# Sliding attention: the two key triangles selected by GpSimd from one ScalarE copy

## The chip, the cores and the metric

The kernel runs on one core of a Trainium2 chip. A core has five engines, each with a queue of its own that it works off in order: TensorE (PE in the profile; its weight loads are shown as PEld), VectorE (DVE), ScalarE (ACT), GpSimd (POOL) and SyncE (SP, which here only starts DMAs). They meet through semaphores. SBUF is the working memory of 128 partitions; PSUM is where TensorE writes, and GpSimd does not read it in this kernel. The metric is the device time of one execution in microseconds, as the median of several runs.

## The reference

Two residual layers over 256 tokens of width 1024. Each layer projects the normalised stream with one large matrix and feeds three parallel mixers: a state-space scan, a sliding-window attention and a forgetting attention. Their outputs are gated, projected, merged and added to the stream. The change sits in the sliding-window attention. Its queries come in blocks of 128, and each block sees the block of keys before it and its own:

```python
qi = jnp.arange(blk)[:, None]
sj = jnp.arange(2 * blk)[None, :]
diff = qi + blk - sj
band = (diff >= 0) & (diff < SWA_WINDOW)
key_pos = jnp.arange(nb)[:, None, None] * blk - blk + sj[None]
mask = band[None] & (key_pos >= 0)
scores = jnp.where(mask[None, :, None, None], scores, -jnp.inf)
probs = jax.nn.softmax(jnp.concatenate([scores, sink], axis=-1), axis=-1)[..., :-1]
out = jnp.einsum('bnkgqs,bnskd->bnqkgd', probs.astype(v.dtype), vb)
```

With a window of 128 and blocks of 128, the second query block (b = 1) sees a strict triangle of the first key block and the complementary triangle of the second. Together they are exactly 128 keys a query, so the kernel can hold the probabilities of both triangles in one 128x128 square per head.

## The kernel before, in words

**The dense work.** Everything is float32. A large product is made from three: the operands are split into a high part, rounded by ACT to a format that TensorE takes at a higher rate (`hi`, line 293), and a remainder that DVE computes from it (`lo`, line 294, which reads the raw tile and `hi`, both in SBUF). Weights arrive by SP's DMAs of 512 KB into `raw`, are split, and are then multiplied. Results leave PSUM by ACT copies (lines 489 and 490), whose two halves are added by a DMA that POOL issues (line 491, called from `dma_sum`). On DVE the convolution's taps are line 832, and lines 839 and 940 finish gates; all three read two operands in SBUF. On POOL, line 1071 selects a triangle of the forgetting attention's bias.

**The order.** TensorE's order is written out: the program lists its dense products one after the other, and a small planner (`pump`, with a model clock and the due times in the `D_` constants) enters steps of the attention between them. The order on ACT, DVE and POOL is set by the scheduler that builds the program from the data's dependences.

**The sliding attention.** In each layer four groups of four heads go through `attn_quad` with `window=True`. TensorE makes the scores; DVE and ACT make the softmax, and leave the probabilities in `pps[0]` for the first query block and in `pps[1]` for the second. Then the `if window:` part transposes each block on TensorE (line 113), four heads into one PSUM bank `pt`:

- for b = 0, ACT copies the bank into `first[:, 0, :]` (line 676);
- for b = 1, DVE multiplies the bank by `other`, a strict lower triangle of ones, into `first[:, 1, :]` (line 678), and by `tri`, the upper triangle with the diagonal, into `both` (line 679).

`first` holds both query blocks' weights on the first key block, `both` the second query block's weights on the second key block. `products_with_values` multiplies them with the values: per head one product of 256 columns from `first` and one of 128 from `both`. It is done for two groups at once: `pair` collects them, and `values` runs the first group's products into a bank `mx` and the second group's into a bank `mm`. The values tile stands as `bias` in the profile, since it shares that tile's slots. The selects' or masks' results of the first and third group thus wait for the second and fourth.

The lines of the profile are those of this kernel; behind the change, every line from 209 on stands 3 lower (491 becomes 488, 294 becomes 291).

Of the kernel before, what the change touches and what calls it, by code (L numbers as in the profile page):

```python
# [13 lines left out]
AF = mybir.ActivationFunctionType  # L14
ALU = mybir.AluOpType

P = 128
# [33 lines left out]
def hybrid_trunk(  # L51
# [5 lines left out]
    nc = tc.nc  # L57
# [11 lines left out]
    def T(tag, shape, dtype=F32, bufs=None):  # L69
        count[0] += 1  # L70
        return sb.tile(shape, dtype, tag=tag, name=f"{tag}_{count[0]}",
                       bufs=bufs if bufs is not None else BUFS.get(tag, 1))
# [8 lines left out]
    def pmx():  # L81
        return PS("mx", 5)

    act = nc.scalar.activation
    stt = nc.vector.scalar_tensor_tensor
    tt = nc.vector.tensor_tensor
# [24 lines left out]
    def transpose(o, a, i):  # L111
        clock["t"] += 0.109
        nc.tensor.transpose(o, a, i)  # L113
# [74 lines left out]
    for j in range(2):  # L188
# [3 lines left out]
    tri = T("tri", [P, P])  # L192
    nc.gpsimd.memset(tri, 1.0)
    nc.gpsimd.affine_select(out=tri, in_=tri, compare_op=ALU.is_ge, fill=0.0, base=0,
                            pattern=[[1, P]], channel_multiplier=-1)
# [3 lines left out]
                            pattern=[[1, P]], channel_multiplier=-1)  # L199
# [3 lines left out]
    nc.gpsimd.tensor_copy(onesr, one)  # L203
    ones = onesr.bitcast(F32)

    wmask, other = T("wmask", [P, P]), T("other", [P, P])
    nc.gpsimd.memset(wmask, 0.0)
    nc.gpsimd.affine_select(out=wmask, in_=wmask, compare_op=ALU.is_ge, fill=NEG, base=0,
                            pattern=[[-1, P]], channel_multiplier=1)
    nc.gpsimd.memset(other, 1.0)  # L210
    nc.gpsimd.affine_select(out=other, in_=other, compare_op=ALU.is_ge, fill=0.0, base=-1,
                            pattern=[[-1, P]], channel_multiplier=1)
    mhalf = T("mhalf", [P, 8])
    nc.gpsimd.memset(mhalf, -0.5)
# [5 lines left out]
    def bc(ap, axis, n):  # L220
        s = list(ap.shape)
        s.insert(axis, n)
        return ap.unsqueeze(axis).to_broadcast(s)
# [117 lines left out]
    first, late = [], []  # L341
# [244 lines left out]
    def attn_quad(y, last, products, biases, nsink, v, vcols, sz, gated, scored=lambda: None, window=False):  # L586
# [16 lines left out]
        def score(p, i, b):  # L603
            return scs[2 * p + i][:, b * P:P + 2 * P * b]
# [11 lines left out]
        for h in range(4) if window else ():  # L616
            own = pps[0][:, h // 2, h % 2 * P:h % 2 * P + P]
            nc.vector.tensor_tensor_reduce(  # L618
                out=own, in0=scs[h][:, 0:P], in1=wmask, scale=-0.125, scalar=nsink[:, h:h + 1],
# [23 lines left out]
        for p in () if window else range(2):  # L643
            pp = pps[p]
            ps_ = slice(4 * p, 4 * p + 4)
            for i in range(2):
                for b, sl in blocks:
                    e = 4 * p + 2 * i + b
                    nc.vector.tensor_tensor_reduce(  # L649
                        out=pp[:, i, sl], in0=score(p, i, b), in1=biases(p, i, b), scale=-0.125,  # L650
# [15 lines left out]
        if window:  # L666
            first, both = T("L4", [P, 2, 512]), T("L2", [P, 512])
            for b in range(2):
                if b == 1:
                    yield D_SOFT2  # L670
                pt = pmx()
                for h in range(4):
                    transpose(pt[:, h * P:(h + 1) * P], pps[b][:, h // 2, h % 2 * P:h % 2 * P + P], ident)
                ptv = pt.rearrange("p (h q) -> p h q", h=4)
                if b == 0:
                    act(first[:, 0, :], pt, AF.Copy)
                else:
                    tt(first[:, 1, :].rearrange("p (h q) -> p h q", h=4), ptv, bc(other, 1, 4), op=ALU.mult)
                    tt(both.rearrange("p (h q) -> p h q", h=4), ptv, bc(tri, 1, 4), op=ALU.mult)
        else:  # L680
            order = [(0, 0), (0, 1), (1, 0), (1, 1), (0, 2), (1, 2),
                     (2, 0), (2, 1), (2, 2), (3, 0), (3, 1), (3, 2)]
            at = {hb: (n // 4, n % 4 * P) for n, hb in enumerate(order)}
            pTs = []
            for n, (h, b) in enumerate(order):
                if n == 6:
                    yield D_SOFT2
                if n % 4 == 0:
                    pt = pmx()
                transpose(pt[:, n % 4 * P:(n % 4 + 1) * P], pps[h // 2][:, h % 2, b * P:(b + 1) * P], ident)  # L690
                if n % 4 == 3:
                    if n == 3:
                        two = T("L4", [P, 2, 512])
                    pT = T("L2", [P, 512]) if n == 11 else two[:, n // 4, :]
                    act(pT, pt, AF.Copy)
                    pTs.append(pT)
# [42 lines left out]
    def swa_quad(y, g, q):  # L739
        yield lambda: 1 in y.sz  # L740

        def products(score):
            for b in range(2):
                for c in range(2):
                    for h in range(4):
                        r = slice(32 * h, 32 * h + 32)
                        mm(score(h // 2, h % 2, b), q[r, c, b * P:(b + 1) * P], y.kT[r, (h - g) % 4, c, 0:(b + 1) * P],
                           start=(c == 0), stop=(c == 1))

        yield from attn_quad(  # L750
            y, g == 3, products, None, y.nsink[:, 4 * g:4 * g + 4], y.bv,
            lambda p, i: slice(64 * g, 64 * g + 64),
            lambda: y.sz[1][:, 2 * g:2 * g + 2, :], lambda: (1, 2 * g + 1) in y.zdone, window=True)
# [304 lines left out]
    def fox_quad(y, j):  # L1058
# [26 lines left out]
        def scored():  # L1085
            tokens["bias"] += 1

        yield from attn_quad(y, j == 6, products, lambda p, i, b: bs[p][:, i, P * b:P + 2 * P * b], None, y.cv,
                             lambda p, i: slice(P * (j + p) + 64 * i, P * (j + p) + 64 * i + 64),
                             lambda: y.sz[2][:, j:j + 2, :], lambda: (2, j + 1) in y.zdone, scored)  # L1090
# [168 lines left out]
    def sub(src, n=256):  # L1259
        subs.append((src, n))  # L1260
        return len(subs) - 1
# [5 lines left out]
    for y in layers:  # L1267
# [108 lines left out]
        o = [sub([(0, w_out[l, :, c:c + n])], n) for c, n in ((0, 256), (256, 512), (768, 256))]  # L1376
# [43 lines left out]
    with tc.manual_schedule(engines={ENG.PE, ENG.DVE, ENG.Activation, ENG.Pool}):  # L1420
# [11 lines left out]
        p = pmx()  # L1432
# [93 lines left out]
        for i in range(2):  # L1526
# [6 lines left out]
                                op=ALU.add)  # L1533
# [50 lines left out]
```

## Time and profile before

| what | value |
|---|---|
| median of 3 runs | 808.11 us (807.27 to 808.14) |
| the profiled execution, its own time | 808.24 us |
| its span (first to last instruction) | 806.5 us |
| granted TensorE clock | 0.999 |
| PE busy | 797.2 us (99%) |
| DVE busy | 684.8 us (85%), 1414 instructions |
| ACT busy | 533.7 us (66%), 1144 instructions |
| POOL busy | 170.9 us (21%), 238 instructions |

A row of a timeline has the start and the duration in microseconds, the engine, the line, the operation, output<-inputs, sizes, and the number of instructions merged into it; in brackets stands how long the engine was idle before it and what ended that. A row of a line's own view has shortest, median and longest duration in nanoseconds, and the first and last start. A row of waits has the total, the number of waits and the longest. Matmuls overlap, so their durations are longer than the time from one to the next.

### The profile page before, as it was taken

The page shows a single profiled execution, that of the slowest core. Times are in us where ns is not written, and L with a number is a line of the kernel's source. Part 1 is how long each engine was busy: PE and PEld are TensorE (multiplying, and loading weights), DVE is VectorE, ACT ScalarE, POOL GpSimd, SP SyncE. Part 2 cuts the span into 40 slices and gives each one's busy share as a digit, 9 for nine tenths or more (in the row PEclk, how much of TensorE's full clock was granted, in tenths as well). Part 3 has the DMA queues.
Part 4 walks back from the last instruction along what each step waited for, and adds up shares of the span by engine and source line. Part 5 has one row for each costly group of instructions (what it writes and reads, how often), then busy time and mean ns, then how long its engine had stood idle before and what let it go on. Part 6 is the DMA issues. An engine that isn't in the chain of part 4 may idle for free.

```text
span 806.5 us, 14832 instructions
## 1 busy us (share of the span) xinstructions
PE 797.2 (99%) x5162; PEld 711.2 (88%) x5162; DVE 684.8 (85%) x1414; ACT 533.7 (66%) x1144; POOL 170.9 (21%) x238
## 2 busy tenths in 40 slices
PE   8999999999999999999999999999999999999996
PEld 7998988888888988888998899888889989888896
DVE  6868999998899997795785799999879999969865
ACT  7776768875776785543665678687747768755452
POOL 3156213130320100033001741222212110002000
PEclk9999999999999999999999999999999999999999
DMA  9998987797665565676678987689986646576632
GB/s 313 268 266 178 248 222 195 212 295 226 161 212 172 170 192 171 220 249 210 215 245 259 235 206 225 158 217 281 267 229 184 194 147 200 157 248 210 210 109 75
DMA packets 138826, 170.43 MB, mean 211 GB/s; under 512 B 9352, under 2 KB 106464, under 8 KB 138752
## 3 DMA queue, kind: packets, MB, share of 16 engines
q1 hardware_dynamic: 114960, 140.53, 55.3%
q0 software_dynamic: 13328, 13.29, 10.3%
q10 hardware_dynamic: 10464, 15.67, 6.7%
q8 instruction: 41, 0.67, 0.3%
q14 instruction: 33, 0.27, 0.1%
HBM read 154.71 MB, written 2.16 MB: 195 GB/s over the span
## 4 chain that ended last, share of the span: by engine, by line
PE 97%; DVE 1%; DMA 1%; issue 0%; ACT 0%; SPq 0%
PE mm L109 84%; PE mx L109 10%; PE mx L113 3%; DMA raw<-in_w_in_dram 1%; DVE lo L294 0%; DVE L L1102 0%; SPq L189 0%; DVE L L1446 0%; ACT L L1450 0%; ACT hi L1459 0%; ACT L L1226 0%; DVE L L1201 0%; SPq L363 0%; DVE L L1205 0%; DVE L L288 0%
## 5 line engine op out<-in xcount | busy, mean ns | idle before, releaser
L109 PE MATMUL mm<-L,hi 128*128 128x512 f32 x1056 | 354.0, 387 | 0.7 <-DVE L L1102 0.5
L294 DVE TENSOR_TENSOR lo<-raw,hi 128x1024 fp32r<-128x1024 f32 (+1 forms) x276 | 312.4, 1151 | 43.8 <-ACT hi L293 41.1
L293 ACT ACTIVATE hi<-raw 128x1024 fp32r<-128x1024 f32 (+1 forms) x276 | 265.9, 982 | 60.3 <-PE mm L109 38.2
L109 PE MATMUL mm<-hi,L 128*128 128x512 f32 (+2 forms) x1168 | 303.4, 349 | 0.1
L109 PE MATMUL mm<-L,lo 128*128 128x256 f32 x1056 | 266.6, 273 | 0.0
L109 PEld LDWEIGHTS mm<-hi,L 128*128 128x128 f32 x1168 | 205.7, 190 | 23.1 <-issue 1.5
L109 PEld LDWEIGHTS mm<-L,hi 128*128 128x128 f32 x1056 | 194.9, 190 | 27.3 <-issue 4.9
L109 PEld LDWEIGHTS mm<-L,lo 128*128 128x128 f32 x1056 | 202.1, 191 | 5.4
L109 PE MATMUL mm<-lo,L 128*128 128x512 f32 (+2 forms) x584 | 201.6, 347 | 0.0
L109 PEld LDWEIGHTS mm<-lo,L 128*128 128x128 f32 x584 | 110.2, 190 | 11.0 <-DVE lo L294 0.3
L491 POOL DMA_DIRECT2D L<-L x68 | 60.3, 911 | 191.9 <-ACT L L490 180.2
L1071 POOL TENSOR_SCALAR_AFFINE_SELECT bias<-bias 128x128 f32<-128x128 f32 x64 | 33.4, 555 | 77.2 <-DMA bias<-cumd 77.2
L832 DVE SCALAR_TENSOR_TENSOR L<-L,vec,L 128x255 f32<-128x255 f32 (+2 forms) x96 | 46.2, 481 | 2.1 <-ACT L L829 0.3
L489 ACT ACTIVATE L<-mm 128x256 f32<-128x256 f32 x84 | 32.0, 381 | 19.5 <-PE mm L109 14.1
L655 ACT ACTIVATE pp<-pp,nm 128x128 f32<-128x128 f32 x64 | 28.2, 443 | 22.1 <-DVE nm L649 22.1
L1105 ACT ACTIVATE L<-L 128x512 f32<-128x512 f32 x24 | 15.1, 630 | 35.7 <-DVE L L1102 31.2
L491 POOL DMA_DIRECT2D qt<-L x16 | 13.8, 862 | 76.3 <-ACT qt L490 76.3
L613 ACT ACTIVATE pp<-pp,nm 128x128 f32<-128x128 f32 x32 | 12.6, 394 | 25.6 <-DVE nm L618 24.9
L1138 POOL TENSOR_TENSOR L<-L,L 128x512 f32<-128x512 f32 x8 | 12.0, 1496 | 73.9 <-DVE L L1137 73.9
L490 ACT ACTIVATE L<-mm 128x256 f32<-128x256 f32 x68 | 26.2, 386 | 1.2 <-DMA L<-L 1.2
L1102 DVE TENSOR_TENSOR L<-mm,L 128x512 f32<-128x512 f32 x22 | 15.1, 686 | 11.7 <-PE mm L109 9.1
L838 ACT ACTIVATE L<-L 128x256 f32<-128x256 f32 x32 | 13.4, 418 | 16.5 <-DVE L L832 16.4
(212 smaller groups left out, 918.3 us busy)
## 6 DMA issues: line engine op xcount, KB each, us to landing
raw<-in_w_in_dram SPq DMA_DIRECT2D x191, 512.0 KB, 5.2
raw<-in_w_proj_dram SPq DMA_DIRECT2D x48, 512.0 KB, 6.2
L<-L POOLq DMA_DIRECT2D x72, 128.0 KB, 5.4
raw<-in_w_out_dram SPq DMA_DIRECT2D x16, 512.0 KB, 4.8
bias<-cumd ACTq DMA_DIRECT2D x16, 256.0 KB, 3.2
L<-cumd ACTq DMA_DIRECT2D x8, 512.0 KB, 6.5
L<-in_gate_bias_dram ACTq DMA_DIRECT2D x12, 256.0 KB, 5.9
qt<-L POOLq DMA_DIRECT2D x16, 128.0 KB, 6.0
```

The lines of the kernel that those rows point to most:

```text
L109: nc.tensor.matmul(o, a, b, **kw)
L113: nc.tensor.transpose(o, a, i)
L293: keep(act)(hi, src, AF.Copy)
L294: keep(tt)(lo, src, hi.bitcast(F32), op=ALU.subtract)
L489: act(halves(lo), ordered(p[:, S:2 * S]), AF.Copy)
L490: last = act(halves(out), ordered(p[:, 0:S]), AF.Copy)
L491: nc.gpsimd.dma_start(out, lo, accum_op=ALU.add)
L655: act(pp[:, i, sl], pp[:, i, sl], AF.Exp, scale=-1.0, bias=nm[:, e:e + 1], accum_out=sums[:, e:e + 1])
L832: stt(a[:, s:S], x_[:, 0:S - s], y.vec[:, 16 * j + u:16 * j + u + 1], a[:, s:S], op0=ALU.mult, op1=ALU.add)
L1071: nc.gpsimd.affine_select(out=bias[:, i, dst], in_=bias[:, i, src], compare_op=ALU.is_ge, fill=NEG, base=0, pattern=[[-1, P]], channel_mul ...
L1102: tt(halves(g), p, halves(y.gb), op=ALU.add)
L1105: finish(act(g, g, AF.Tanh, scale=0.5))
```

## The change

ACT now copies the transposed bank for both query blocks, so that the second block's square lands whole in `first[:, 1, :]`. Two GpSimd instructions then select the triangles in SBUF: the first reads `first[:, 1, :]` and writes `both` with zeros below the diagonal's triangle; the second works in place on `first[:, 1, :]` and zeroes the other triangle. Each covers four heads of 128x128 in one instruction (128x512). The second has to wait for the first, since it overwrites what the first reads. The two DVE multiplications go, and so do the `other` tile, its memset and its select.

```diff
-    wmask, other = T("wmask", [P, P]), T("other", [P, P])
+    wmask = T("wmask", [P, P])
     nc.gpsimd.memset(wmask, 0.0)
     nc.gpsimd.affine_select(out=wmask, in_=wmask, compare_op=ALU.is_ge, fill=NEG, base=0,
                             pattern=[[-1, P]], channel_multiplier=1)
-    nc.gpsimd.memset(other, 1.0)
-    nc.gpsimd.affine_select(out=other, in_=other, compare_op=ALU.is_ge, fill=0.0, base=-1,
-                            pattern=[[-1, P]], channel_multiplier=1)
...
-                ptv = pt.rearrange("p (h q) -> p h q", h=4)
-                if b == 0:
-                    act(first[:, 0, :], pt, AF.Copy)
-                else:
-                    tt(first[:, 1, :].rearrange("p (h q) -> p h q", h=4), ptv, bc(other, 1, 4), op=ALU.mult)
-                    tt(both.rearrange("p (h q) -> p h q", h=4), ptv, bc(tri, 1, 4), op=ALU.mult)
+                act(first[:, b, :], pt, AF.Copy)
+            heads = [o.rearrange("p (h q) -> p h q", h=4) for o in (first[:, 1, :], both)]
+            nc.gpsimd.affine_select(out=heads[1], in_=heads[0], compare_op=ALU.is_ge, fill=0.0, base=0,
+                                    pattern=[[0, 4], [1, P]], channel_multiplier=-1)
+            nc.gpsimd.affine_select(out=heads[0], in_=heads[0], compare_op=ALU.is_ge, fill=0.0, base=-1,
+                                    pattern=[[0, 4], [-1, P]], channel_multiplier=1)
```

TensorE's and SP's orders are the same in both kernels. On the other three engines the scheduler places the new instructions, and shifts some neighbours by a few places. Two places matter; at both, layer 1 stands like layer 0.

The first place is the last of the four groups. ACT before (`mx_2187` is the transposed bank, `qt` a tile of the forgetting attention's queries and keys, `L_502` a split of the gated output):

```order
L838 ACTIVATE L_443_2162<-L_430_2115 128x256
L489 ACTIVATE L_446_2183<-mm_2166 128x256
L490 ACTIVATE qt_2165<-mm_2166 128x256
L293 ACTIVATE L_502_2448<-L_182_905 128x2x256 x2
L293 ACTIVATE hi_2293<-raw_2068 128x1024
```

ACT after (`L_430` is now `first`):

```order
L835 ACTIVATE L_442_2162<-L_429_2115 128x256
L486 ACTIVATE L_445_2183<-mm_2166 128x256
L487 ACTIVATE qt_2165<-mm_2166 128x256
L671 ACTIVATE L_430_2120<-mx_2187 128x512
L290 ACTIVATE L_501_2449<-L_181_902 128x2x256 x2
L290 ACTIVATE hi_2294<-raw_2068 128x1024
```

The copy stands behind the eviction of `qt`, and the splits come one place later. POOL there before:

```order
L491 DMA L_434_2128<-L_442_2158 128x256
L491 DMA qt_2165<-L_446_2183 128x256
L491 DMA qt_2194<-L_456_2224 128x256
L491 DMA L_458_2233<-L_460_2251 128x256
L491 DMA L_465_2283<-L_473_2313 128x256
```

POOL there after (`L_431` is `both`):

```order
L488 DMA L_433_2128<-L_441_2158 128x256
L488 DMA qt_2165<-L_445_2183 128x256
L673 AFFINE_SELECT L_431_2121<-L_430_2120 128x512
L675 AFFINE_SELECT L_430_2120<-L_430_2120 128x512
L488 DMA qt_2195<-L_455_2225 128x256
L488 DMA L_457_2234<-L_459_2252 128x256
```

The two selects stand between two DMA issues for `qt`. DVE there before:

```order
L294 TENSOR_TENSOR lo_2219<-raw_2056,hi_2218 128x1024
L839 TENSOR_SCALAR L_377_1862<-L_443_2162,L_430_2115 128x256
L678 TENSOR_TENSOR L_431_2120<-mx_2187,other_89 128x512
L679 TENSOR_TENSOR L_432_2121<-mx_2187,tri_76 128x512
L294 TENSOR_TENSOR L_503_2449<-L_182_905,L_502_2448 128x2x256
L294 TENSOR_TENSOR lo_2294<-raw_2068,hi_2293 128x1024
```

DVE there after:

```order
L291 TENSOR_TENSOR lo_2220<-raw_2056,hi_2219 128x1024
L836 TENSOR_SCALAR L_376_1861<-L_442_2162,L_429_2115 128x256
L291 TENSOR_TENSOR L_502_2450<-L_181_902,L_501_2449 128x2x256 x2
L291 TENSOR_TENSOR lo_2295<-raw_2068,hi_2294 128x1024
L829 TENSOR_SCALAR L_456_2229<-L_425_2090,vec_891,L_456_2229 128x255
```

The masks are gone, and the two remainders of the gated output, which read two SBUF operands each, follow line 836 directly.

The second place is the second group. POOL before:

```order
L491 DMA L_307_1528<-L_315_1558 128x256
L491 DMA L_182_905<-L_319_1589 128x256
L491 DMA L_182_905<-L_327_1622 128x256
L491 DMA L_343_1711<-L_345_1729 128x256
L491 DMA L_351_1752<-L_359_1782 128x256
```

POOL after:

```order
L488 DMA L_306_1526<-L_314_1556 128x256
L673 AFFINE_SELECT L_293_1455<-L_292_1454 128x512
L675 AFFINE_SELECT L_292_1454<-L_292_1454 128x512
L488 DMA L_181_902<-L_318_1588 128x256
L488 DMA L_181_902<-L_326_1621 128x256
```

The selects stand right behind the DMA issue for `L_306`; the DMAs for the gate tile `L_181` come after them.

## The prediction

> **What bounds the kernel now.** I read the page's totals first, then the chain that ended last, then the waits of TensorE.
>
> ```profile
> span 806.5 us, 14832 instructions
> PE 797.2 (99%) x5162; PEld 711.2 (88%) x5162; DVE 684.8 (85%) x1414; ACT 533.7 (66%) x1144; POOL 170.9 (21%) x238
> ...
> PE 97%; DVE 1%; DMA 1%; issue 0%; ACT 0%; SPq 0%
> ...
> PE mx L113 <- POOL ident masks.py:199: 1.5, 1, 1.5
> PE mx L109 <- ACT hi L1459: 0.6, 2, 0.3
> PE mm L109 <- DVE L L1102: 0.5, 1, 0.5
> ...
> 799.95 0.28 PE L109 MATMUL mm<-lo,L 128*128 128x256 f32 x1
> ```
>
> The chain that ended last is PE for 97%. PE is busy 797.2 of 806.5 us, so it is idle for 9.3. Of that, 1.5 are ahead of the first matmul, 806.5 - 800.2 = 6.3 lie behind the last one, and 0.6 are start-up waits for ACT. About 0.9 us are left for the whole middle, 0.5 of them one wait for DVE. The order of PE's instructions is the same in both kernels. So whatever VectorE is spared, at most about 0.9 us can come back (somewhat more if the modelled ends of matmuls hide part of a wait: 0.5 on top is my allowance). A loss has no such limit: a late operand at an in-order engine that is 99% busy is paid in full.
>
> **What goes, what comes.** Eight head groups (four in each of two layers) each lose two DVE masks and gain one ACT copy and two POOL selects.
>
> ```profile
> L676 ACT ACTIVATE L<-mx x8: 593/600/656, 80.6 to 548.4; 128x512 f32<-128x512 f32 x8
> L678 DVE TENSOR_TENSOR L<-mx,other x8: 670/680/685, 85.4 to 554.6; 128x512 f32<-128x512 f32 x8
> L679 DVE TENSOR_TENSOR L<-mx,tri x8: 674/684/689, 86.3 to 555.2; 128x512 f32<-128x512 f32 x8
> ```
>
> DVE: 8 x (0.68 + 0.68) = 10.9 us less. ACT: 8 x 0.60 = 4.8 us more. The PSUM bank of the transposed block is then read by one engine once, which frees it no later than two masks did: nothing. The removed `other` (a memset and a select on POOL in the first 4 us) has no one waiting for it: nothing.
>
> POOL: 16 selects of 128x512, a size that the trace does not have. Its neighbours:
>
> ```profile
> 2.48 0.20 POOL L207 MEMSET wmask<- 128x128 f32 x1
> 3.02 0.29 POOL L211 TENSOR_SCALAR_AFFINE_SELECT other<-other 128x128 f32<-128x128 f32 x1
> 3.26 0.10 POOL L214 MEMSET mhalf<- 128x8 f32 x1
> ...
> 52.58 0.73 POOL L564 TENSOR_TENSOR L<-L,L 128x256 f32<-128x256 f32 x1
> 55.29 0.58 POOL L574 DMA_DIRECT2D L<-L  x1 [0.30 <-POOL L L565]
> 337.30 1.28 POOL L1138 TENSOR_TENSOR L<-L,L 128x512 f32<-128x512 f32 x1 [22.27 <-DVE L L1137]
> ```
>
> Memsets grow by 0.10 us for 120 columns, 0.0008 each: the select would be 0.29 + 384 x 0.0008 = 0.60. The other end is the 1.28 of a two-input operation of the same size. Those grow by (1.28 - 0.73) / 256 = 0.0021 a column with two inputs, half of that with one, and 0.29 + 384 x 0.0011 = 0.70 is what I take, since it rests on rows that read as well as write. The second select overwrites what the first reads, so it waits for it: 0.30 us, as L574 waited for L565. A pair costs 0.70 + 0.30 + 0.70 = 1.7 us when nothing is in its way.
>
> [...]
>
> **What is in the selects' way.** Two-input VectorE work on SBUF and POOL work hold each other up.
>
> ```profile
> 53.28 1.71 POOL L565 TENSOR_TENSOR L<-L,L 128x256 f32<-128x256 f32 x1
> 53.15 1.24 DVE L294 TENSOR_TENSOR lo<-raw,hi 128x1024 fp32r<-128x1024 f32 x1 [1.71 <-ACT hi L293]
> 54.32 0.95 DVE L554 TENSOR_TENSOR L<-L,cs 128x256 f32<-128x256 f32 x1
> L554 DVE TENSOR_TENSOR L<-L,cs x40: 410/418/1914, 48.7 to 471.8; 128x256 f32<-128x256 f32 x40
> ...
> 218.31 2.35 DVE L294 TENSOR_TENSOR lo<-raw,hi 128x1024 fp32r<-128x1024 f32 x2
> 218.55 2.60 POOL L1071 TENSOR_SCALAR_AFFINE_SELECT bias<-bias 128x128 f32<-128x128 f32 x1 [2.81 <-DMA bias<-cumd]
> ```
>
> L565 sat through L294 and then ran while L554, normally 0.42, took 0.95. So a POOL operation waits for the DVE one under way, and the next DVE one pays up to 0.53. Sixteen selects can take back 16 x 0.53 = 8.5 of DVE's 10.9 us. And the 0.29 us select at 218.55 took 2.60: it outlasted both L294 (to 220.66), the second of which started after it had asked.
>
> [...]
>
> **Where somebody waits for the selects.** TensorE multiplies them with the values two head groups at a time. The first of each pair is made over 20 us ahead: hidden. The second of each pair is not. The last group of layer 0 (engines in turn: ACT, POOL, DVE, PE; then layer 1):
>
> ```profile
> 158.35 0.39 ACT L490 ACTIVATE qt<-mm 128x256 f32<-128x256 f32 x1
> 158.61 0.65 ACT L293 ACTIVATE L<-L 128x512 fp32r<-128x512 f32 x1
> ...
> 159.03 0.86 POOL L491 DMA_DIRECT2D qt<-L  x1 [1.89 <-ACT qt L490]
> ...
> 159.24 0.42 DVE L839 SCALAR_TENSOR_TENSOR L<-L,L 128x256 f32<-128x256 f32 x1
> 160.18 0.68 DVE L679 TENSOR_TENSOR L<-mx,tri 128x512 f32<-128x512 f32 x1
> 160.78 0.68 DVE L294 TENSOR_TENSOR L<-L,L 128x512 fp32r<-128x512 f32 x1
> ...
> 161.70 1.47 PE L109 MATMUL mm<-L,bias 128*64 128x256 f32 x16
> ...
> 555.23 0.68 DVE L679 TENSOR_TENSOR L<-mx,tri 128x512 f32<-128x512 f32 x1
> 556.74 0.60 PE L109 MATMUL mm<-L,bias 128*64 128x256 f32 x4
> ```
>
> Today the second mask ends at 160.86 and PE reads at 161.70: 0.84 us spare; in layer 1 556.74 - 555.91 = 0.83. In the new order the copy stands behind L490, in the place of L293 at 158.61, and ends at 159.21. The selects stand behind the DMA issue of 159.03, so POOL is free at 159.89. On DVE, L839 ends at 159.66 and L294 follows at once, at about 159.75 because the copy delays its ACT half by about 0.5; it runs to 160.43. Select 1 waits for it: 160.43 to 161.13. In the 0.30 us before select 2 the other L294 of this size gets in: to 161.80. Select 2 ends at 162.50, and PE starts 0.8 late. Twice: +1.6 us. The ends of this term: 159.89 + 1.7 = 161.59 if nothing blocks, no loss; the two blocked cases among the rivals are the upper end.
>
> The second group of layer 0:
>
> ```profile
> 107.82 0.39 ACT L490 ACTIVATE L<-mm 128x256 f32<-128x256 f32 x1
> 108.50 0.86 POOL L491 DMA_DIRECT2D L<-L  x1 [1.42 <-ACT L L490]
> 109.05 0.48 DVE L832 SCALAR_TENSOR_TENSOR L<-L,vec,L 128x253 f32<-128x253 f32 x1
> 112.92 0.39 PE L109 MATMUL mm<-L,bias 128*64 128x256 f32 x2
> ```
>
> The copy follows L490 (to 108.7), POOL is free at 109.36, DVE's L832 ends at 109.53: select 1 to 110.23. A full L294 (1.22, held up until then) gets in: to about 111.4, select 2 to 112.1. PE reads at 112.92. Hidden, with 0.8 us spare, and gone if a select costs 0.4 more.
>
> **What DVE's relief buys.** Its one large wait in the middle, 0.5 us at L1102, comes some 15 us behind the masks of the third group:
>
> ```profile
> 135.03 0.68 DVE L678 TENSOR_TENSOR L<-mx,other 128x512 f32<-128x512 f32 x1
> 135.20 0.42 ACT L838 ACTIVATE L<-L 128x256 f32<-128x256 f32 x1 [1.39 <-DVE L L832]
> 135.65 0.43 DVE L839 SCALAR_TENSOR_TENSOR L<-L,L 128x256 f32<-128x256 f32 x1
> ```
>
> L678 filled a hole there: L839 had to wait for L838 until 135.62 anyway. What is left is one mask (0.68) against up to two blocked operations (2 x 0.53): DVE between 0.7 earlier and 0.4 later. I take 0.3 of the possible 0.9 us over both layers; the ends are 0 and 1.4.
>
> ACT's later splits and the DMA issues that now stand behind selects cost nothing: the waits for a split in the body are a few tenths in all,
>
> ```profile
> PEld mm L109 <- DVE lo L294: 0.3, 1, 0.3
> 206.14 2.97 PE mx L109 x40
> ```
>
> and the q/k sum issued next on POOL (161.56 today, about 1 us later then) is first read by the score matmuls at 206.
>
> **Sum.** +1.6 - 0.3 = +1.3 us. The profiled execution took 808.24 (span 806.5 and 1.7 around it), 0.13 above the median of 808.11: 809.5 against the one, 809.4 against the median.
>
> **Rivals.**
> - Granted at once. POOL slips in ahead of L294 both times: selects end at 161.59, within the 0.84 spare. Against it: DVE has two-input work back to back there. -0.6 to +0.3 us, about 807.9.
> - Starved, as at 218.55: select 1 from 159.89 to 162.49, select 2 behind the rest of a long L294 to 164.0 or later, PE 2.3 or more late in each layer: 2 x 2.3 - 0.3 = +4.3, 812.4 or more.
> - A dear select of 1.28. Last group: 160.43 + 1.28, L294 to 162.39, + 1.28 = 163.67, 2.0 late. Second group: 113.3 against 112.92, 0.4 late. 2 x 2.4 - 0.3 = +4.5, 812.6.
> - Faster. DVE's 10.9 us reach PE: this needs the selects done by 161.70 and, beyond that, waits of PE that its busy time does not show. With all of 0.9 + 0.5 recovered it is 806.7, still within 0.2%; beyond that only what I do not see.
> - The change does not do what it says: no; the masks are gone from DVE's order and the selects stand in POOL's. Rather, a delayed DMA behind a select could surface elsewhere; the rows above leave it over 40 us.
>
> **Numbers.** 0.2% is 1.6 us, about what a measurement of this kernel can tell from no change. Blocked once per pair (likeliest): 0.42, at +0.3 to +2.0 us (808.4 to 810.1), 0.27 of it within 0.2% and 0.15 above. Granted at once: 0.18, within. Starved 0.13, dear select 0.12, a late DMA or ACT 0.05: slower. Hidden elsewhere, no change: 0.03. Faster: 0.07. Together: faster 0.07, within 0.48, slower 0.45. The range 807.4 to 812.7 leaves out the faster case, the best of the granted one and the worst of the starved one.
>
> **What would show it.** Right: DVE's busy time down by 2 to 6 us and not by 10.9; POOL up by 16 selects of 0.7 to 2 us; ACT up by 4.8; a wait of PE for POOL at the value matmuls of the second pair in both layers, 0.4 to 1 us each, and none at the first pair; the L1102 wait still there. Wrong: no PE wait for POOL at all; selects well over 1.3 us with DVE idle; or a PE wait at a place that reads neither masks nor selects.

## The result, and the profile after

The changed kernel takes 811.38 us (810.81 to 811.88) against 808.01 (807.27 to 808.45) for the one before, run beside it: ratio 1.0044, 95% interval 1.0034 to 1.0054. It is 3.4 us slower. The prediction's range holds that, its likeliest case (809.4, own range to 810.1) does not.

The totals of the profile after, and its chain that ended last:

```profile
span 809.3 us, 14839 instructions
PE 797.1 (98%) x5162; PEld 710.9 (88%) x5162; DVE 684.4 (85%) x1398; ACT 537.5 (66%) x1152; POOL 185.7 (23%) x252
...
PE 84%; DVE 9%; ACT 3%; issue 3%; DMA 1%; SPq 0%; ACTq 0%; DVEq 0%
```

TensorE's waits (us in total, times, longest):

```profile
PE mm L109 <- DVE L L1099: 2.1, 2, 1.2
...
PE mx L113 <- DVE sums L636: 1.2, 2, 0.7
PE mm L109 <- DVE L L723: 0.5, 2, 0.3
```

PE works as long as before, but now waits 2.1 + 1.2 + 0.5 = 3.8 us for DVE in the middle of the span, where it waited 0.5. These 3.3 us more are the bulk of the result: set matmul against matmul, TensorE in the profile after is 0.9 us ahead of the one before at 30 us, from the start-up, and 2.8 us behind at the end. None of the three places reads a mask or a select itself: L1099 (before: L1102) adds the bias to a gate's projection, L636 closes the softmax of the sliding attention, L723 takes value products out of PSUM. DVE lost 16 masks and is as busy as before (684.8, now 684.4); its share of the chain rose from 1% to 9%.

The groups of the new instructions (busy us, mean ns):

```profile
L671 ACT ACTIVATE L<-mx 128x512 f32<-128x512 f32 x16 | 9.8, 613 | 0.0
L673 POOL TENSOR_SCALAR_AFFINE_SELECT L<-L 128x512 f32<-128x512 f32 x8 | 7.1, 882 | 4.5 <-ACT L L671 4.5
L675 POOL TENSOR_SCALAR_AFFINE_SELECT L<-L 128x512 f32<-128x512 f32 x8 | 6.1, 760 | 0.5
```

An undisturbed select of the first group, and POOL and DVE about the two of the second, in order of time:

```profile
85.73 0.64 POOL L675 TENSOR_SCALAR_AFFINE_SELECT L<-L 128x512 f32<-128x512 f32 x1
...
107.62 0.86 POOL L488 DMA_DIRECT2D L<-L  x1 [1.42 <-ACT L L487]
108.04 0.22 DVE L781 SCALAR_TENSOR_TENSOR L<-L 128x64 f32<-128x64 f32 x1
108.17 0.97 POOL L673 TENSOR_SCALAR_AFFINE_SELECT L<-L 128x512 f32<-128x512 f32 x1
108.17 1.25 DVE L829 SCALAR_TENSOR_TENSOR L<-L,vec,L 128x253 f32<-128x253 f32 x1
109.21 0.71 POOL L675 TENSOR_SCALAR_AFFINE_SELECT L<-L 128x512 f32<-128x512 f32 x1
109.35 0.65 DVE L781 SCALAR_TENSOR_TENSOR L<-L 128x64 f32<-128x64 f32 x1
```

A select that nobody disturbs takes 0.64 us. The record of the first one here is 0.97 long because it starts while that of the DMA issue ahead of it still runs (to 108.48); it ends 0.66 us behind that. So both selects run at once, 0.07 us apart, and DVE pays: L829 ends 0.28 us behind the end of the first select, L781 0.08 behind the second's. What follows on DVE is one chain up to PE's wait at 124 us; its pieces (start, duration):

```profile
108.26 0.07 DVE L L829
108.33 1.02 issue
109.35 0.65 DVE L L781
110.00 1.13 DVE lo L291
...
119.49 0.26 DVE pp L615
...
124.09 0.08 DVE sums L636
...
124.23 0.63 PE mx L113 x4
```

The chain books the blocked time as "issue". DVE is busy nearly without a gap from there to the softmax at L615 (11.03 of the 11.20 us from 108.30 to 119.50), so what it loses at 108 can arrive at PE 16 us later; the first experiment shows how much does.

The third and fourth groups of the layer, again POOL, DVE and PE:

```profile
135.22 1.62 DVE L836 SCALAR_TENSOR_TENSOR L<-L,L 128x256 f32<-128x256 f32 x1 [0.54 <-ACT L L835]
135.60 0.95 POOL L673 TENSOR_SCALAR_AFFINE_SELECT L<-L 128x512 f32<-128x512 f32 x1
136.62 0.71 POOL L675 TENSOR_SCALAR_AFFINE_SELECT L<-L 128x512 f32<-128x512 f32 x1
136.76 1.36 DVE L829 SCALAR_TENSOR_TENSOR L<-L,vec,L 128x255 f32<-128x255 f32 x2
...
159.85 0.97 POOL L673 TENSOR_SCALAR_AFFINE_SELECT L<-L 128x512 f32<-128x512 f32 x1
160.04 2.37 DVE L291 TENSOR_TENSOR L<-L,L 128x512 fp32r<-128x512 f32 x2
160.88 0.98 POOL L675 TENSOR_SCALAR_AFFINE_SELECT L<-L 128x512 f32<-128x512 f32 x1
161.97 0.82 PE L109 MATMUL mm<-L,bias 128*64 128x256 f32 x8
```

L836 takes 1.62 us instead of 0.42, the two L291 together 2.37 instead of about 1.3. The values' products, at which the prediction put its loss, start behind the selects without a wait for them, 0.11 us after the second one's end (161.86).

### The profile page after: what moved, and what is told of

Its sections match the earlier page's. It is cut to its first block, busy times and chain, and to the rows that moved or that the text cites. A ratio compares the mean times of both kernels' runs of the same rounds, so it can differ in the third digit from the quotient of the medians.

```text
span 809.3 us, 14839 instructions
## 1 busy us (share of the span) xinstructions
PE 797.1 (98%) x5162; PEld 710.9 (88%) x5162; DVE 684.4 (85%) x1398; ACT 537.5 (66%) x1152; POOL 185.7 (23%) x252
## 4 chain that ended last, share of the span: by engine, by line
PE 84%; DVE 9%; ACT 3%; issue 3%; DMA 1%; SPq 0%; ACTq 0%; DVEq 0%
PE mm L109 73%; PE mx L109 8%; PE mx L113 3%; DVE lo L291 3%; DVE L L829 2%; ACT pp L610 1%; ACT hi L290 1%; DMA raw<-in_w_in_dram 1%; DVE pp L639 1%; DVE L L781 0%; DVE L L723 0%; ACT L L835 0%; ACT L L826 0%; DVE pp L615 0%; DVE L L291 0%
## 5 line engine op out<-in xcount | busy, mean ns | idle before, releaser
L291 DVE TENSOR_TENSOR lo<-raw,hi 128x1024 fp32r<-128x1024 f32 (+1 forms) x276 | 313.0, 1154 | 45.7 <-ACT hi L290 41.4
L109 PEld LDWEIGHTS mm<-lo,L 128*128 128x128 f32 x584 | 110.2, 190 | 10.7
L829 DVE SCALAR_TENSOR_TENSOR L<-L,vec,L 128x255 f32<-128x255 f32 (+2 forms) x96 | 49.4, 514 | 2.1 <-ACT L L826 0.3
L1102 ACT ACTIVATE L<-L 128x512 f32<-128x512 f32 x24 | 15.1, 631 | 35.2 <-DVE L L1099 30.7
L979 POOL TENSOR_TENSOR sm<-sm,mhalf 128x8 f32<-128x8 f32 x2 | 3.4, 1683 | 95.0 <-DVE sm L977 95.0
```

What stands on the lines that cost most here:

```text
L109: nc.tensor.matmul(o, a, b, **kw)
L291: keep(tt)(lo, src, hi.bitcast(F32), op=ALU.subtract)
L829: stt(a[:, s:S], x_[:, 0:S - s], y.vec[:, 16 * j + u:16 * j + u + 1], a[:, s:S], op0=ALU.mult, op1=ALU.add)
L1102: finish(act(g, g, AF.Tanh, scale=0.5))
```

## The experiments

The theory after reading the trace: a select on GpSimd and a VectorE operation with two SBUF operands exclude each other; VectorE loses to the selects all that the masks had freed, and its lateness reaches TensorE through softmax and evictions. Rivals: the scheduler's new order on VectorE, which puts splits ahead of softmax and evictions; ScalarE's copies. TensorE's order is the same in all kernels below, but for a few value products in the run with cut selects. Times are set against runs of the kernel before beside them (medians 807.85 to 807.98).

**The changed kernel without its selects.**

```diff
-            first, both = T("L4", [P, 2, 512]), T("L2", [P, 512])
+            first = T("L4", [P, 2, 512])
...
-            nc.gpsimd.affine_select(out=heads[1], in_=heads[0], ...)
-            nc.gpsimd.affine_select(out=heads[0], in_=heads[0], ...)
...
-                            m = both[:, h * P:(h + 1) * P] if b else first[:, :, h * P:(h + 1) * P]
+                            m = first[:, 1, h * P:(h + 1) * P] if b else first[:, :, h * P:(h + 1) * P]
```

> The changed kernel without its 16 selects: the value products of both blocks read ScalarE's unmasked copy (so the output is not the reference's). VectorE's and TensorE's written orders are those of the changed kernel. Theory (the selects hold VectorE up): VectorE's busy time falls to about 674 (684.4 less the 10.9 us of masks), TensorE's new waits behind L636, L1099 and L723 go, and the time is 807 to 808.3. Rival 1 (VectorE's written order, which moved splits ahead of softmax and evictions): VectorE falls to 674 too, but TensorE's waits at 124, 152 and 169 us stay, and the time is 810 to 811.5. Rival 2 (ScalarE's 4.8 us of copies): the same as rival 1.

Measured: 806.48 us, ratio 0.9982 (0.9973 to 0.9990), 0.5 us below the range that the theory gave. Its totals and its chain:

```profile
PE 796.2 (99%) x5162; PEld 711.7 (88%) x5162; DVE 676.8 (84%) x1398; ACT 537.6 (67%) x1152; POOL 168.5 (21%) x236
...
PE 98%; DMA 1%; DVE 0%; ACT 0%; SPq 0%; issue 0%
```

The tap that stood at 108.17:

```profile
108.58 0.48 DVE L824 SCALAR_TENSOR_TENSOR L<-L,vec,L 128x253 f32<-128x253 f32 x1
```

VectorE's instructions stand in the same order as in the changed kernel, so both rivals fall: new order, copies and fewer masks together make the kernel 1.5 us faster, and the 16 selects alone cost 811.38 - 806.48 = 4.9 us. Since the order is the same, each VectorE operation can be set against its twin: fourteen that meet a select take 0.22 to 1.20 us longer, 7.7 us in all; busy time differs by 7.6. TensorE's waits behind VectorE are gone, the 0.5 of the kernel before too.

The twins also show how the loss travels. In layer 0 VectorE of the changed kernel ends its operations 0.41 us ahead of this one until 108 us, 0.80 behind after the second group's selects and still 0.82 behind at L636 (124 us), 2.32 behind after the third group's and 2.35 at L1099 (151 us), 3.18 behind after the fourth's and at L723 (168 us). It loses at the selects, and next to nothing is added or made good between them. TensorE, set matmul against matmul, falls 0.6, 1.4 and 0.5 us further behind at these three places and 0.9, 1.0 and 0.5 in layer 1: 4.9 us, the whole difference.

**Masks kept, selects added to the kernel before.**

```diff
+                    spare = T("spare", [P, 448])
+                    nc.gpsimd.affine_select(out=spare, in_=first[:, 1, 0:448], ...)
+                    nc.gpsimd.affine_select(out=spare, in_=spare, ...)
```

> The kernel before, its masks and its written order on VectorE and ScalarE kept, and beside them two selects (448 columns, into a tile that nobody reads) on GpSimd behind each pair of masks. Theory (the selects hold VectorE up): VectorE's busy time rises from 684.8 by 4 to 11 us, waits of TensorE behind VectorE appear as in the changed kernel, and the time is 810 to 813. Rivals 1 and 2 (written order; copies): neither is changed here, so at most 808.5.

Measured: 809.22 us, ratio 1.0017 (1.0008 to 1.0026), VectorE 687.3. Slower, which the rivals excluded, but short of both ranges of the theory: here ten VectorE operations lose 0.17 to 0.36 us, 2.7 in all, and in each layer one select loses 3.0. Two places:

```profile
85.78 0.68 POOL L681 TENSOR_SCALAR_AFFINE_SELECT spare<-L 128x448 f32<-128x448 f32 x1 [2.23 <-DVE L L678]
85.96 0.67 DVE L679 TENSOR_TENSOR L<-mx,tri 128x512 f32<-128x512 f32 x1
...
110.83 3.53 POOL L683 TENSOR_SCALAR_AFFINE_SELECT spare<-spare 128x448 f32<-128x448 f32 x1
110.86 0.41 DVE L844 SCALAR_TENSOR_TENSOR L<-L,L 128x256 f32<-128x256 f32 x1
111.19 0.22 DVE L789 SCALAR_TENSOR_TENSOR L<-L 128x64 f32<-128x64 f32 x1
111.33 1.21 DVE L294 TENSOR_TENSOR lo<-raw,hi 128x1024 fp32r<-128x1024 f32 x1
112.46 0.21 DVE L789 SCALAR_TENSOR_TENSOR L<-L 128x64 f32<-128x64 f32 x1
112.60 1.22 DVE L294 TENSOR_TENSOR lo<-raw,hi 128x1024 fp32r<-128x1024 f32 x1
```

At 85.96 the mask, which reads one operand from the matmul bank, runs under a select in its usual time (0.67 us; 0.68 in the kernel before). At 110.83 a select sits out five VectorE operations, each with two SBUF operands, each of usual length: it takes 3.53 us.

**Memsets in the place of the selects.**

```diff
-            nc.gpsimd.affine_select(out=heads[1], in_=heads[0], ...)
-            nc.gpsimd.affine_select(out=heads[0], in_=heads[0], ...)
+            for _ in range(3):
+                nc.gpsimd.memset(first[:, 1, :], 0.0)
```

> The changed kernel with three memsets of the copied block on GpSimd (estimate from the 128x128 row of 0.2 us: 0.4 to 0.5 us each) in the place of the two selects, which write and read nothing (the block is zero then, so the output is not the reference's). Theory in its narrow form (a select holds VectorE up because it reads and writes its operands): VectorE stays near 674, 807 to 808.3. In its wide form (any long GpSimd operation does): VectorE near 680 to 685, 810 to 811.5. Rival 1 (written order): 810 to 811.5 with VectorE at 674.

As in the run without selects, all products read the copied block.

Measured: 806.93 us, ratio 0.9985 (0.9976 to 0.9994), VectorE 676.5. The group of the memsets:

```profile
L673 POOL MEMSET L<- 128x512 f32 x24 | 14.6, 608 | 5.4 <-ACT L L671 4.5
```

The same place:

```profile
108.94 2.02 POOL L673 MEMSET L<- 128x512 f32 x3
108.95 0.48 DVE L826 SCALAR_TENSOR_TENSOR L<-L,vec,L 128x253 f32<-128x253 f32 x1
```

GpSimd is busy with them for 14.6 us, longer than with the selects (13.2), and VectorE keeps its 0.48. The narrow form holds. It also settles a rival that the prediction named, a DMA issued late behind the selects: behind the memsets of the third group the next DMA issue stands as late (at 137.15 us; 137.46 behind the selects, 136.55 without either), and nothing is lost.

**Plain copies in the place of the selects.**

```diff
+            for _ in range(2):
+                nc.gpsimd.tensor_copy(both, first[:, 1, :])
```

> The changed kernel with two plain GpSimd copies of the copied block into the second tile in the place of the selects (nothing is masked, so the output is not the reference's). Theory (it is the reading of SBUF by GpSimd that holds VectorE up, not the select): VectorE's busy time near 684, 810.5 to 812, the waits behind L636, L1099 and L723 are there. Rival (something of the select itself): VectorE near 677, 806.5 to 807.3, as with the memsets.

Measured: 811.03 us, ratio 1.0035 (1.0023 to 1.0048), VectorE 683.3. The waits:

```profile
PE mm L109 <- DVE L L1096: 1.4, 2, 0.8
PE mx L113 <- DVE sums L636: 1.1, 2, 0.6
...
PE mm L109 <- DVE L L720: 0.4, 2, 0.2
```

The same places as with the selects. So in this kernel it is GpSimd's reading of SBUF that holds VectorE up, and a copy does it as a select does: against the run with neither (VectorE 676.8 us), the memsets, which only write, cost VectorE nothing (676.5), the copies 6.5 us and the selects 7.6. The tap that takes 0.48 us beside the memsets takes 1.21 beside the copies and 1.25 beside the selects. The mask at 85.96, with one operand from the matmul bank, kept its time.

**ScalarE's copy, with both masks multiplied from it.**

```diff
-            nc.gpsimd.affine_select(out=heads[1], in_=heads[0], ...)
-            nc.gpsimd.affine_select(out=heads[0], in_=heads[0], ...)
+            tt(heads[1], heads[0], bc(tri, 1, 4), op=ALU.mult)
+            tt(heads[0], heads[0], bc(other, 1, 4), op=ALU.mult)
```

> ScalarE copies the transposed block once, and VectorE multiplies both masks, from the copy instead of from the matmul bank; no selects. Theory: VectorE's busy time stays at 684 to 686, ScalarE's rises by 4.8, the masks end about 0.6 us later than before, within the 0.83 us that the value products leave: 807.8 to 809. Rival 2 (the copies cost it): 810 or more. VectorE's written order lies between the two kernels', so rival 1 gives 808 to 811.

The tile `other` is made at the start again.

Measured: 808.40 us, ratio 1.0004 (0.9995 to 1.0012), VectorE 684.9. The copies cost nothing that can be told from no change.

**One select instead of two.**

```diff
+            if t == 1:
+                gtt(y.bv[:, 1, :], y.bv[:, 1, :], y.bv[:, 0, :], op=ALU.subtract)
...
-            nc.gpsimd.affine_select(out=heads[0], in_=heads[0], ...)
```

> One select a head group instead of two. It uses V0'P_other + V1'P_tri = V0'P + (V1 - V0)'P_tri: the first block's values read ScalarE's unmasked copy, only the second triangle is selected, and one GpSimd subtraction a layer (128x256) turns the second block of values into the difference. VectorE's written order is that of the changed kernel. Theory (VectorE waits out the selects that it meets): about half the loss of 4.9 us goes, VectorE's busy time near 680, 808.5 to 809.5. Rival (any select in that place costs the whole): 811. Rival (only two in a row cost something): 806.5 to 807.3.

Measured: 809.60 us, ratio 1.0019 (1.0010 to 1.0028), VectorE 681.9. The first select, with the subtraction, costs 809.60 - 806.48 = 3.1 us, a little above the half that was expected, and the second 1.8.

**Each select cut into four.**

```diff
+            for h in range(4):
+                nc.gpsimd.affine_select(out=heads[1][:, h, :], in_=heads[0][:, h, :], ...)
+            for h in range(4):
+                nc.gpsimd.affine_select(out=heads[0][:, h, :], in_=heads[0][:, h, :], ...)
```

> The changed kernel with each select cut into four of 128x128 (about 0.29 us each by the rows of the masks at the start). If a VectorE operation waits for one GpSimd instruction at a time, it loses at most 0.3 us to each meeting, VectorE's busy time is 679 to 682 and the time 808 to 810 (the values may then come late). If it waits until GpSimd stops, it waits for all eight (2.3 us or more): VectorE 686 or more, 812 to 815.

Measured: 815.37 us, ratio 1.0091 (1.0077 to 1.0105). VectorE came out as the first branch said (681.3; no operation loses over 0.18 us), the time as the second, and for another reason: now the selects starve. The second four in the line's own view (shortest, median, longest in ns):

```profile
L677 POOL TENSOR_SCALAR_AFFINE_SELECT L<-L x32: 283/1162/1772, 86.9 to 562.3; 128x128 f32<-128x128 f32 x32
```

The last group of the layer, POOL and PE:

```profile
158.91 3.44 POOL L674 TENSOR_SCALAR_AFFINE_SELECT L<-L 128x128 f32<-128x128 f32 x4
161.90 2.86 POOL L677 TENSOR_SCALAR_AFFINE_SELECT L<-L 128x128 f32<-128x128 f32 x4
162.93 0.65 PE L109 MATMUL mm<-L,bias 128*64 128x256 f32 x2 [1.72 <-POOL L L677]
```

And TensorE's wait:

```profile
PE mm L109 <- POOL L L677: 4.6, 4, 1.7
```

A 0.28 us select has a median record of 1.16, since VectorE operations get in between one and the next (and since records of neighbours overlap, which counts some of the waiting twice). The eight end at 164.76, where two whole ones ended at 161.86, and TensorE waits for them at the values. VectorE's small losses add no wait. 4.6 us of the 8.9 by which this kernel is slower than the one without selects are such waits. The rest lies mostly in the same place: matmul against matmul, TensorE falls behind that kernel by 3.2 us at the last group's value products of layer 0 and by 4.6 at those of layer 1 and just behind them, 7.8 in all. The mean granted clock of the profiled execution was 0.996, against 0.999 in that of the changed kernel; why layer 1 loses more than layer 0 stays open.

**One mask, no select.** The identity of the run with one select, on the kernel before; the mask stays on VectorE.

```diff
+            if t == 1:
+                gtt(y.bv[:, 1, :], y.bv[:, 1, :], y.bv[:, 0, :], op=ALU.subtract)
...
-                if b == 0:
-                    act(first[:, 0, :], pt, AF.Copy)
-                else:
-                    tt(first[:, 1, :].rearrange("p (h q) -> p h q", h=4), ptv, bc(other, 1, 4), op=ALU.mult)
+                act(first[:, b, :], pt, AF.Copy)
+                if b == 1:
                     tt(both.rearrange("p (h q) -> p h q", h=4), ptv, bc(tri, 1, 4), op=ALU.mult)
```

> The same identity as the run with one select, but the one triangle is multiplied by VectorE, from the matmul bank, and there is no select: VectorE 8 masks fewer than before, ScalarE 8 copies more. Theory: VectorE's busy time falls to about 680 (684.8 less 5.4, and little comes back, since no select meets it), no new wait of TensorE, 806.3 to 807.6: faster than both kernels or level with the one before. Rival (the removed masks were worth nothing at all in time, only the written order of the runs without selects): 807.8 to 808.4.

Measured: 806.42 us, ratio 0.9982 (0.9974 to 0.9991): faster than both kernels. Its chain is PE for 99%, no wait for VectorE is left, and its VectorE is busier (682.8) than expected and than that of the run without selects (676.8) at the same time: beyond some relief, VectorE's load buys nothing here.

**One select added to that order, beside the mask.**

```diff
+            nc.gpsimd.affine_select(out=heads[0], in_=heads[0], ...)
```

> One select and one mask a head group, no identity: ScalarE copies the block, VectorE multiplies the second triangle from the matmul bank, GpSimd selects the first triangle in the copy. VectorE's, ScalarE's and TensorE's written orders are those of the run with one mask; the select is all that is added to it. Theory in its present form (only VectorE operations with two SBUF operands stand against a select; the mask reads one operand from the matmul bank, so the select runs under it): part of the 3.1 us that a select a group cost without such a mask is saved, 807 to 808.8, and the mask keeps its 0.68 us beside the select. Rival (any VectorE work beside a select suffers): 809 to 810, with masks of more than 0.9 us.

Measured: 810.17 us, ratio 1.0031 (1.0019 to 1.0043). The masks keep their length, as expected; the time misses the expectation. The group of the masks:

```profile
L673 DVE TENSOR_TENSOR L<-mx,tri 128x512 f32<-128x512 f32 x8 | 5.5, 683 | 0.1
```

The second group of layer 0:

```profile
108.78 1.26 DVE L830 SCALAR_TENSOR_TENSOR L<-L,vec,L 128x253 f32<-128x253 f32 x1
108.79 0.97 POOL L676 TENSOR_SCALAR_AFFINE_SELECT L<-L 128x512 f32<-128x512 f32 x1
```

In four of the eight groups the select does not run beside the mask: in the second group of a layer it comes 3 us before it, in the third 0.3 to 0.6 us behind it, and it meets a tap or a gate instead, as in the changed kernel. Set against their twins in the run with one mask, those four operations lose 0.77, 0.78, 0.88 and 1.20 us and two splits 0.24 each: 4.1 us of VectorE, for 810.17 - 806.42 = 3.75 us of time. (Busy time differs by 2.3 alone, since three splits far from any of these selects, at 22, 338 and 424 us, had been 1.2 us longer in the run with one mask; two of them met that run's GpSimd subtraction.) In this stretch a microsecond of VectorE is nearly a microsecond of the kernel.

## Why the prediction was right and wrong

- **The range.** It holds 811.4 by luck. Above 810.1 it was drawn for selects that starve (812.4 or more) or cost 1.28 us each (812.6), and neither happened; the case that did happen, selects granted at once, was put at 807.9.
- **The bound.** Right: PE sets the time, the gain is small and a loss is paid in full. The most that could come back was put at 0.9 us and 0.5 on top; without the selects 1.5 came back.
- **The select's price.** Right: 0.64 us undisturbed, between the 0.60 and the 0.70 of the two estimates. The second select follows after 0.07 us, not 0.30.
- **The values' wait, +1.6 us: the step that failed in the sum.** It had select 1 wait for a split on DVE and a second split slip in between. In the run the DMA issue ahead of select 1 came 0.27 us later than reckoned (159.30, not 159.03) and its record ended at 160.16; select 1 ended 0.66 us behind it, at 160.82, with no wait for the split, and the splits waited. (That its record starts at 159.85, close to the reckoned 159.89, is chance.) The selects ended at 161.86; TensorE, by then 0.27 us later itself (161.97, not 161.70), waited for nothing, with 0.11 us to spare where 0.84 had been. This term is 0, not 1.6.
- **"What DVE's relief buys", -0.3 us: the term with the wrong sign.** It allowed 0.53 us to a blocked operation and asked about one wait only. Measured are up to 1.20 us to one operation, and 7.6 us of busy time taken back. Of the masks' 10.9, busy time shows only 8.0 without the selects, though the operations' durations, added up, fall by 10.7: the records of neighbours overlap by about 0.1 us (L781 ends at 108.26, where L829 has started at 108.17), and busy time counts that once. So nothing was left, where 2 to 6 us were forecast, and in time the term is not -0.3 but about +3.4, the whole result. At the third group DVE was to be between 0.7 us early and 0.4 late; L836 and the L829 behind it lost 1.56.
- **"ACT's later splits ... cost nothing"** holds for the copies. But the slack was read from TensorE's own waits, and these say little of how close a chain of DVE work behind them is to being late.
- **The rivals.** "Granted at once" is what happened to the selects, and its price was wrong: a select that is granted is paid by DVE (L829 at 108.17 took 1.25 us instead of 0.48). "Starved" is real as well: cut selects showed it, with 815.4 us. "Dear select" did not occur. "Faster" is what the change would do with no selects in it: 806.48, reckoned 806.7.
- **The signs named.** No TensorE wait for POOL, and waits at places that read neither masks nor selects: two of the three signs that were to say "wrong" came. The growth of the L1102 wait from 0.5 to 2.1 us was not foreseen. ACT's busy time rose by 3.8, not 4.8.

## What to carry to other kernels

Work that moves from VectorE to GpSimd must be priced on VectorE too. Here VectorE operations with two SBUF operands that met a select (0.64 us undisturbed) took 0.22 to 1.20 us longer, fourteen of them 7.7 us in all, while memsets in the same place cost VectorE nothing. So count such meetings, and follow VectorE's chain to the next point where the bounding engine reads it. Cutting each select into four lowered VectorE's busy time from 684.4 to 681.3 us and shifted the wait to GpSimd and to the reader of its result: TensorE waited 4.6 us. Better than moving the work was removing it: one subtraction a layer replaced half of the masks.

## What was not expected of the hardware

- Who waits does not follow from the recorded starts. L836 started at 135.22, 0.38 us ahead of the select's record, and lost 1.20 us. At 110.83 in the run with masks and selects, the select started while L789 (110.72) was under way and 0.03 us ahead of L844, and sat out four more operations as well: 3.53 us. L829 at 108.17 sat out a whole select: it ended at 109.42, 0.28 us behind select 1. Which of the two came first can't be read here, since a recorded start is not the moment at which an instruction gets its operands: select 1's record at 108.17 starts 0.31 us before the DMA issue ahead of it on its own engine ends. What decides between the two stays open.
- A longer record of a GpSimd instruction need not mean that it met VectorE. A memset that starts before the record of a DMA issue ends is 0.85 to 0.87 us long where the others are 0.52, and a first select in the same position 0.95 to 0.97 instead of 0.64: about the 0.3 us of the overlap in both cases. Of the changed kernel's selects only the second of the last group is much longer without such an overlap (0.98 at 160.88), beside a split on VectorE.
